# Two-layer hybrid backbone on one core: the token shift of the RWKV in-projection by transfers inside SBUF and one blend, low-rank weights padded to 128 rows

## The chip, the cores and the metric

One core of a Trainium2 chip runs the whole program in one launch. The metric is the device time of one execution in microseconds; lower is better. The work runs on TensorE (PE in the rows, its weight loads PEld), VectorE (DVE), ScalarE (ACT), GpSimd (POOL), and the DMA engines, which are fed mostly from SyncE's queue (SP). Each engine, and SP's queue too, takes its instructions strictly in the order of the program.

## What is computed

1024 latent tokens (a grid of 16 rows of 64) and 256 context tokens pass through two layers. The first has an in-projection of 1024 to 3840 channels; its first 2560 columns are mixed with a shifted copy of themselves, and this mixing is what the change rewrites:

```python
def qshift(u, rows):                       # latent tokens
    g = u.reshape(b, rows, GRID_W, ch // 4, 4)
    left  = jnp.pad(g[:, :, :-1, :, 0], ...)   # channel 0 of 4: neighbour to the left
    right = jnp.pad(g[:, :, 1:, :, 1], ...)    # channel 1: to the right
    up    = jnp.pad(g[:, :-1, :, :, 2], ...)   # channel 2: one grid row up
    down  = jnp.pad(g[:, 1:, :, :, 3], ...)    # channel 3: one grid row down
...
        s = (s + (shift_fn(s) - s) * mu).astype(jnp.float32)
        r, k0, v, wl_f, wl_b, al_f, al_b = jnp.split(s, cuts, axis=-1)
...
    w_log = -jax.nn.softplus(-(w0 + jnp.tanh(wl) @ w2)) - 0.5
    a = jax.nn.sigmoid(a0 + al @ a2)
```

The context uses the same with two classes of channels (previous and next token). Channels lie on the partitions, tokens along the free axis, so a class of channels is every fourth (or every second) partition and a shift is an offset along the row. The low-rank inputs `wl`, `al` have 64 channels for each of the two directions.

## The kernel before

The first part of the program (phase A, up to about 590 us) is the in-projection. A tile of 128 output channels is one product: 8 steps of 9 matmuls (three operand splits of fp32 into two parts, three blocks of 256, 512 and 512 tokens; lines 546 to 553). Two PSUM tiles of such a product are live at a time (pool `pg`). `gemm(plan)` (in `phaseA`) issues a product and, after the steps that the plan names, work for other tiles; this plan fixes the order on every engine by hand.

The order of products is: 18 and 19 (the low-rank inputs), 28, 29 (gates), 26, 27 (Fourier), then for each of six pairs of heads p the tiles k, v, r; then the last gates. For a pair, in the loop at the end of `phaseA` (`P` is the new pair, `old` the one before):

- in the product of the new k: `old.take(0, pr)` mixes r, then `operands(0, 0)`, `operands(0, 1)` build the forward operands of the state update, `values` turns v by TensorE (`pvt`, line 757, copied by ACT at 758) and stores it to DRAM in six transfers (lines 763 to 765);
- in the product of v (`VPL`): `B` splits the low-rank weights (`wsplit`: `hw`, `ha` on ACT, then `lw`, `la` on VectorE, line 727) and mixes k (`take(1, k)`); `l` issues low-rank products (`lora`, lines 779 and 780, their tanh on ACT at 781); `q` is `square` (ACT, line 740), `o` are the backward operands `operands(1, .)`. Then `norm` (matmuls `pn`, line 746) reads the squares;
- in the product of r (`RPL`): more `lora`, `b` the bonus (`pbo`, line 866, multiplied on VectorE at 867), `t` mixes v (`take(2, v)`), `T` and `S` send the norms through DRAM (`RN`, line 792) and back spread over the partitions (`kk`, line 800), which `keys` multiplies at 806.

`norm`, `lora` and the bonus share two PSUM buffers (`gen`), so `pbo` can start only when `rn` (VectorE, line 748) has read `pn`. On VectorE `rn` stands behind all of `operands(1, .)`. On ACT `square` stands ahead of the exponentials `Pp`, `Pi` (832, 833) of `operands(1, .)`.

`mix` (line 560) takes a product from PSUM: two ACT instructions write `m = (1 - mu) * u` (564, 565), then six VectorE passes add `mu` times the shifted PSUM tile, each with a column of multipliers (`muc`) that is zero outside one class of channels (line 575). For the low-rank inputs ACT also copies the PSUM tile to `u` first (568, 569), and the passes read that. `lowrank` then applies the tanh (for 18 only) and `stacked` splits the tile into two parts (ACT 540, VectorE 541).

A `lora` product is `wh` (both halves of the 128 partitions hold the 64 rows of a direction, 128 rows) times the stacked input, plus the rest `wl` of the weights (64 rows, `w[hs, :]`) times one half of the input (lines 779, 780).

Around the low-rank inputs SP also loads 1 MB pieces of the modulation weights (`aw`, line 314) with two small loads each (line 320); product 29 is followed by matmuls on these pieces (`pada`, line 331) in the two `gen` buffers, which ACT empties into `adap` (333). In ACT's order the split of `AL` (540), two weight casts (528) and the gate of product 28 (590, 591) stand ahead of these copies.

Weights of a product come in two halves of 256 KB (`wr`, line 521), each loaded two halves ahead. The build gives the DMAs of SP's queue eight semaphores in turn; each DMA waits until the one issued eight before it has landed.

Of the kernel before, what the change touches and what calls it, by code (L numbers as in the profile page):

```python
# [18 lines left out]
T = 1280  # L19
# [27 lines left out]
KT = 4  # L47
# [34 lines left out]
def host_consts():  # L82
# [16 lines left out]
    c["cls"] = np.stack([t % 4 == 0, t % 4 == 1, t % 4 == 2, t % 4 == 3, t % 2 == 0, t % 2 == 1], 1)  # L99
# [114 lines left out]
def setup(g, es):  # L214
    nc, tc = g.nc, g.tc
    cp = es.enter_context(tc.tile_pool(name="cp", bufs=1, reuse_waits="tile"))
    g.cp = cp
    es.enter_context(tc.manual_schedule())
    load_consts(g, ["cols", "ident"], cp)
    c = g.K["cols"]  # L220
    g.col = lambda n: c[:, COLS[n][0] : COLS[n][0] + COLS[n][1]]
    mh = cp.tile([128, 1], F32, name="mhalf")
    nc.gpsimd.memset(mh, -0.5)
    g.K["mhalf"] = mh
    one = cp.tile([128, 1], F32, name="one")
    nc.gpsimd.memset(one, 1.0)
    g.K["one"] = one
    g.dv = cp.tile([128, 6 + 6 + 6 + 6 + 12 + 12 + 20 + 120], F32, name="dv")
    g.ap = cp
    g.shc = cp.tile([128, 2, 8, 2], F32, name="shc")  # L230
    g.scc = cp.tile([128, 2, 8, 2], F32, name="scc")


def derived(g):
# [5 lines left out]
    def sl(n):  # L240
# [186 lines left out]
def front(g, A, load, split, steps):  # L427
# [3 lines left out]
    with ExitStack() as es:  # L431
# [3 lines left out]
        for t in range(10):  # L435
# [8 lines left out]
            if t == 1:  # L444
                load_consts(g, ["cls", "sel2"], g.cp)
                derived(g)
                ada_setup(g, A.wp)
# [255 lines left out]
class Pair:  # L703
# [63 lines left out]
    def lora(self, d):  # L767
# [104 lines left out]
def phaseA(g, B=None):  # L872
# [72 lines left out]
    load_consts(g, ["fch", "selh", "onesbd", "mscan"], g.lp)  # L945
# [29 lines left out]
    load_consts(g, ["fctx"], g.fp)  # L975
# [10 lines left out]
    v = gemm({i: [some(F1, 1)] for i in range(1, 7)})  # L986
# [4 lines left out]
    for p in range(g.npair + 1):  # L991
        P = P if not p else Pair(g, p) if p < g.npair else None
        if old:
            val, bon = old.values(), old.bonus()
            first = lambda: (old.take(0, pr), old.kdir())
            k = gemm({0: [first], 4: [lambda: old.operands(0, 0), some(val, 1)], 5: [some(val, 1)], 6: [lambda: old.operands(0, 1), some(val, 2)]})
        if P:
            lo0, lo1, keys = P.lora(0), P.lora(1), P.keys()
        if not old:
# [3 lines left out]
            pr = gemm({0: [lambda: P.take(2, v)], 1: [some(lo0, 2)], 2: [some(lo0, 2)], 3: [some(lo0, 2)], KT: [P.turned, some(lo1, 2)], KF: [P.spread, some(lo1, 2)], 6: [some(lo1, 2)], 7: [some(keys, 4)]})  # L1003
        elif P:
            def act(a, n):
                return {"B": lambda: (P.wsplit(), P.take(1, k)), "l": some(lo0, n), "q": P.square, "o": lambda: old.operands(1, n), "u": old.sum_dirs, "p": old.store_pc, "b": some(bon, n)}[a]
# [3 lines left out]
            def act(a, n):  # L1010
                return {"l": some(lo1, n), "b": some(bon, n), "k": some(keys, n), "t": lambda: P.take(2, v), "T": P.turned, "S": P.spread}[a]
# [1206 lines left out]
```

## Time and profile before

| | us |
|---|---|
| three runs | 1917.75, 1933.57, 1937.59 (median 1933.57) |
| the profiled execution | 1926.12 |
| its span, first to last instruction | 1924.3 |
| TensorE busy in it | 1779.5 (92%) |
| VectorE busy in it | 1128.5 (59%) |
| ScalarE, GpSimd busy | 716.3, 693.8 |
| mean granted TensorE clock | 0.970 of full speed |

Times in the rows are microseconds from the span's start, mean durations of one instruction are ns where a row says so. A busy TensorE is not one at its peak: its ends are modelled, and only the spacing of starts tells the rate.

### The profile page before, as it was taken

The numbers are of one execution on the slowest core, as the hardware profiler recorded it, in microseconds if no ns is written. First come the engines' busy times: TensorE is split into PE (matmuls) and PEld (weight loads), VectorE is DVE, ScalarE is ACT, GpSimd is POOL, SyncE is SP. The second block draws the span as 40 slices with busy tenths as digits, with TensorE's granted clock in tenths as the row PEclk, the third lists the DMA queues.
The fourth block names the chain that finished last, engine by engine and source line by source line (L and its number), as shares of the span: only waits on it lengthen the run. The fifth ranks groups of instructions, "written<-read, shape, count | busy, mean of one in ns | idle before, by whom it ended". The sixth has DMA issues, their size and how long they took to land. (4 is left out here: it accounts for less than half of the span.)

```text
span 1924.3 us, 38535 instructions
## 1 busy us (share of the span) xinstructions
PE 1779.5 (92%) x15490; PEld 1487.0 (77%) x15490; DVE 1128.5 (59%) x2030; ACT 716.3 (37%) x1598; POOL 693.8 (36%) x826
## 2 busy tenths in 40 slices
PE   6999998999889888989998787999999999999998
PEld 4777776677668777778877676779889898898876
DVE  5532578887884656977888754554352533423643
ACT  5322554544441133455555565343221222212231
POOL 4331334443442414554565522122342424413310
PEclk9999999999999988999999898999999999999999
DMA  9671265556568385678767764433111101101162
GB/s 314 174 238 51 80 173 141 153 141 167 147 164 253 105 187 147 172 176 202 186 181 169 198 178 139 145 123 107 36 56 34 49 30 45 55 34 55 50 202 99
DMA packets 341494, 257.60 MB, mean 134 GB/s; under 512 B 109964, under 2 KB 292740, under 8 KB 341060
## 3 DMA queue, kind: packets, MB, share of 16 engines
q1 hardware_dynamic: 326756, 221.96, 42.3%
q10 hardware_dynamic: 10512, 18.62, 3.2%
q0 software_dynamic: 4048, 14.55, 2.0%
q8 instruction: 123, 2.02, 0.5%
q14 instruction: 55, 0.45, 0.1%
HBM read 175.20 MB, written 79.88 MB: 133 GB/s over the span
## 5 line engine op out<-in xcount | busy, mean ns | idle before, releaser
L552 PE MATMUL pgm<-hh,wh 128*128 128x512 f32 (+1 forms) x624 | 172.9, 386 | 0.0
L530 POOL TENSOR_TENSOR wl<-wr,wh 128x512 fp32r<-128x512 f32 x60 | 85.5, 1430 | 210.3 <-ACT wh L528 190.1
L552 PE MATMUL pgm<-hl,wh 128*128 128x512 f32 (+1 forms) x624 | 160.5, 366 | 0.0
L552 PE MATMUL pgm<-hh,wl 128*128 128x512 f32 (+1 forms) x624 | 159.8, 365 | 0.0
L1138 PE MATMUL psc<-arr,bkp 128*128 128x128 f32 x960 | 136.2, 290 | 9.8 <-DMA bkp<-scr_BK 5.1
L1138 PEld LDWEIGHTS psc<-arr,bkp 128*128 128x128 f32 x960 | 118.5, 196 | 17.9 <-DVE scr L1139 9.1
L552 PEld LDWEIGHTS pgm<-hl,wh 128*128 128x128 f32 x624 | 106.4, 194 | 20.0 <-POOL hl L488 0.9
L552 PEld LDWEIGHTS pgm<-hh,wl 128*128 128x128 f32 x624 | 106.6, 194 | 19.5
L552 PEld LDWEIGHTS pgm<-hh,wh 128*128 128x128 f32 x624 | 99.3, 193 | 27.5 <-issue 14.6
L1872 PE MATMUL pv<-wv,hh 128*128 128x256 f32 x640 | 117.2, 285 | 0.0
L575 DVE SCALAR_TENSOR_TENSOR m<-pgm,dv,m 128x255 f32<-128x255 f32 (+2 forms) x108 | 105.1, 987 | 12.5 <-ACT m L565 9.8
L1139 DVE TENSOR_TENSOR scr<-psc,mask 128x512 f32<-128x512 f32 x120 | 81.8, 685 | 43.3 <-PE psc L1138 42.7
L1872 PEld LDWEIGHTS pv<-wv,hh 128*128 128x128 f32 x640 | 99.5, 192 | 0.1
L1192 DVE TENSOR_TENSOR td<-z,tl 128x70 f32<-128x70 f32 (+40 forms) x248 | 85.0, 343 | 23.0 <-DMA tl<-dn 17.2
L1507 POOL TENSOR_TENSOR state<-tmp,pc 128x256 f32<-128x256 f32 x46 | 36.8, 801 | 167.2 <-DVE tmp L1502 127.1
L1195 DVE TENSOR_TENSOR z<-z,td 128x70 f32<-128x70 f32 (+40 forms) x248 | 88.4, 357 | 8.5
L1438 ACT COPY wt<-ws 64x256 f32<-64x256 f32 x120 | 44.0, 366 | 127.3 <-PE ws L1433 117.7
L1872 PE MATMUL pv<-wv,hl 128*128 128x256 f32 x320 | 90.5, 283 | 0.0
L1611 PE MATMUL pow_eo<-w_eo,yhw_eo 128*128 128x512 f32 x320 | 89.6, 401 | 0.5 <-ACT w_eo L1577 0.4
L1192 POOL TENSOR_TENSOR tp<-z,tl 128x24 f32<-128x24 f32 (+22 forms) x189 | 78.1, 413 | 12.4
L1195 POOL TENSOR_TENSOR z<-z,tp 128x24 f32<-128x24 f32 (+22 forms) x189 | 76.9, 407 | 14.8
L1433 PE MATMUL ws<-vu,scr 128*64 128x64 f32 x960 | 49.5, 230 | 27.4 <-DVE vu L1506 12.4
(339 smaller groups left out, 4286.6 us busy)
## 6 DMA issues: line engine op xcount, KB each, us to landing
aw<-ada_w SPq DMA_DIRECT2D x16, 1024.0 KB, 11.5
wr<-w_ev SPq DMA_DIRECT2D x60, 256.0 KB, 4.2
scr_AR<-ar SPq DMA_DIRECT2D x24, 640.0 KB, 3.8
scr_BK<-bk SPq DMA_DIRECT2D x24, 640.0 KB, 4.5
arr<-scr_AR SPq DMA_DIRECT2D x60, 256.0 KB, 3.8
bkp<-scr_BK SPq DMA_DIRECT2D x120, 128.0 KB, 4.4
br<-scr_BK ACTq DMA_DIRECT2D x60, 256.0 KB, 3.9
x<-xin SPq DMA_DIRECT2D x20, 512.0 KB, 4.4
```

The costliest lines, as they stand in the source:

```text
L530: nc.gpsimd.tensor_tensor(out=wl, in0=wr, in1=wh.bitcast(F32), op=ALU.subtract)
L552: g.nc.tensor.matmul(ps[:, b, :n], lhsT=st[:, k % 4, :], rhs=mv[:, k, c0 : c0 + n], start=(k == 0 and i == 0), stop=(k == 7 and i == 2))
L575: nc.vector.scalar_tensor_tensor(out=o, in0=i, scalar=g.muc[:, q, ft : ft + 1], in1=o, op0=ALU.mult, op1=ALU.add)
L1138: mm(ps[:, 128 * x : 128 * x + 128], lhsT=BK[s][:, h, x, :], rhs=AR[s][:, x, :], start=True, stop=True)
L1139: tt(out=sc[:, :, h].rearrange("p (d q) t -> p d q t", q=2), in0=ps.rearrange("p (d q t) -> p d q t", q=2, t=128), in1=K["mask2"].unsqueez ...
L1192: eng.tensor_tensor(out=tv, in0=Z[:, ra - r0 : rb - r0, s : s + 1].broadcast_to([U, k, n]), in1=TL[:, s : s + 1, s + 1 : 32].broadcast_to( ...
L1195: eng.tensor_tensor(out=zo, in0=zo, in1=tv, op=ALU.add)
L1433: mm(WS[H[h], 64 * x : 64 * x + 64], lhsT=sc[:, x, h, 0:64], rhs=vu[:, x, h], start=True, stop=True, tile_position=(0, 64 * h))
L1438: nc.scalar.copy(WT2[H[h], h].rearrange("p x v -> p (x v)"), WS[H[h], 0:256])
L1507: (nc.vector if SE[0] <= s < SE[1] or s >= SE[2] else nc.gpsimd).tensor_tensor(out=STS[1 - s % 2], in0=tmp, in1=pc.broadcast_to([128, 4, 6 ...
L1611: self.g.nc.tensor.matmul(ps[:, 512 * b : 512 * b + 512], lhsT=st[:, k, :], rhs=mv[:, 512 * b : 512 * b + 512], start=(k == 0 and i == 0), ...
L1872: mm(ps[:, 256 * e : 256 * e + 256], lhsT=st[:, k, c0 : c0 + 128], rhs=mv[:, k, :], start=(k == 0 and i == 0), stop=(k == 7 and i == 2))
```

## The change

`mix` now copies the product from PSUM to `m` unscaled (ACT, two instructions), and six DMAs on SP's queue move the classes of channels, shifted, from `m` into one tile `sh` (128 partitions, 1280 columns, one buffer for all mixes): two of 32 partitions with 16 pieces of 63 elements (252 bytes), two of 32 partitions with 960 elements, two of 64 partitions with 255 elements. A new function `blend` then forms `m = m * (1 - mu)` and `m = sh * mu + m` in two VectorE instructions over 1280 columns. For the pairs `blend` is placed some steps behind `take` (`x` in the plans); for the low-rank inputs it follows at once. `sh` is cleared once, so its borders stay zero.

The rest weights `lw`, `la` become tiles of 128 rows for each direction, cleared once; `wsplit` writes the 64 rows of a direction, and the matmul at line 780 reads all 128 rows. The constant `cls` and the multipliers `muc` go, `fch` is loaded later, and the scratch for DMA descriptors is set to 8192.

```diff
-RPL = {2:"l1",3:"b4 t",4:"l1",5:"T l1",6:"S l2",7:"l1 k4"}
+RPL = {2:"l1",3:"b4 t",4:"l1",5:"T l1 x",6:"S l2",7:"l1 k4"}
-VPL = {0:"B",2:"l2",3:"l2",4:"l2 q o0",5:"u",6:"o1 p"}
+VPL = {0:"B",2:"l2 x",3:"l2",4:"l2 q o0",5:"u",6:"o1 p"}
...
-def mix(g, ps, ft, m, u=None):
+def mix(g, ps, ft, m):
+    nc, sh = g.nc, g.SH
+    pc, pl = ps
+    nc.scalar.copy(m[:, 256:T], pl)
+    nc.scalar.copy(m[:, 0:256], pc)
+    def rows(t, q, n=4):
+        return t[q::n]
+    def grid(t, q):
+        return rows(t, q)[:, 256:T].rearrange("p (r w) -> p r w", w=64)
+    move = nc.sync.dma_start
+    move(grid(sh, 0)[:, :, 1:64], grid(m, 0)[:, :, 0:63])
+    move(grid(sh, 1)[:, :, 0:63], grid(m, 1)[:, :, 1:64])
+    move(rows(sh, 2)[:, 320:T], rows(m, 2)[:, 256 : T - 64])
+    move(rows(sh, 3)[:, 256 : T - 64], rows(m, 3)[:, 320:T])
+    move(rows(sh, 0, 2)[:, 1:256], rows(m, 0, 2)[:, 0:255])
+    move(rows(sh, 1, 2)[:, 0:255], rows(m, 1, 2)[:, 1:256])
+def blend(g, ft, m):
     nc = g.nc
...
-    add(mc[:, 1:256], pc[:, 0:255], 4)
-    add(mc[:, 0:255], pc[:, 1:256], 5)
-    add(mlr[:, :, 1:64], plr[:, :, 0:63], 0)
-    add(mlr[:, :, 0:63], plr[:, :, 1:64], 1)
-    add(ml[:, 64:1024], pl[:, 0:960], 2)
-    add(ml[:, 0:960], pl[:, 64:1024], 3)
+    nc.vector.tensor_scalar(out=m, in0=m, scalar1=g.omm[:, ft : ft + 1], scalar2=None, op0=ALU.mult)
+    nc.vector.scalar_tensor_tensor(out=m, in0=g.SH, scalar=g.col("mu")[:, ft : ft + 1], in1=m, op0=ALU.mult, op1=ALU.add)
...
-            wl = g.sm.tile([128, 128], F32R, tag="l" + n, name=f"l{n}_{self.p}", bufs=1)
+            wl = g.LW[n]
...
-                nc.vector.tensor_tensor(out=wl[a], in0=w[a], in1=wh[a, d].bitcast(F32), op=ALU.subtract)
+                nc.vector.tensor_tensor(out=wl[a, d], in0=w[a], in1=wh[a, d].bitcast(F32), op=ALU.subtract)
...
-                nc.tensor.matmul(pa[:, :bn], lhsT=w[hs, :], rhs=src[hs, b0 : b0 + bn], start=False, stop=True)
+                nc.tensor.matmul(pa[:, :bn], lhsT=w[:, d], rhs=src[:, b0 : b0 + bn], start=False, stop=True)
...
     def lowrank(ps, ft, nm):
         m = g.mp.tile([128, T], F32, tag=f"m{ft % 2}", name=f"m{ft}")
-        mix(g, ps, ft, m, g.mp.tile([128, T], F32, tag="m2", name=f"u{ft}"))
+        mix(g, ps, ft, m)
+        blend(g, ft, m)
...
-            k = gemm({0: [first], 4: [lambda: old.operands(0, 0), some(val, 1)], 5: [some(val, 1)], 6: [lambda: old.operands(0, 1), some(val, 2)]})
+            k = gemm({0: [first], 2: [lambda: old.blend(0)], 4: [lambda: old.operands(0, 0), some(val, 1)], 5: [some(val, 1)], 6: [lambda: old.operands(0, 1), some(val, 2)]})
...
-    nc = bacc.Bacc("TRN2", target_bir_lowering=False, num_devices=1)
+    nc = bacc.Bacc("TRN2", target_bir_lowering=False, num_devices=1, dynamic_dma_scratch_size=8192)
```

The first place is SP's queue where one pair's forward operands and values are stored (`scr_BK`, `scr_VT`; `wr` are halves of weights). Before, the two loads of weights follow the values, whose three rows stand twice in a row:

```order
L850 DMA scr_BK<-bk_0_1_2426 128x10x128
L763 DMA scr_VT<-vt_2386 640x1x128
L764 DMA scr_VT<-vt_2386 64x2x128
L765 DMA scr_VT<-vt_2386 64x8x128
L521 DMA wr_0_2454<-w_ev 128x512
L521 DMA wr_1_2540<-w_ev 128x512
L849 DMA scr_AR<-ar_1_0_2573 128x10x128
```

In the changed program the six moves of `take(1, k)` (the tile `m_2_2492` of pair 2) stand at the same place:

```order
L850 DMA scr_BK<-bk_0_1_2435 128x10x128
L764 DMA scr_VT<-vt_2395 640x1x128
L765 DMA scr_VT<-vt_2395 64x2x128
L766 DMA scr_VT<-vt_2395 64x8x128
L516 DMA wr_0_2463<-w_ev 128x512
L569 DMA sh<-m_2_2492 32x16x63
L570 DMA sh<-m_2_2492 32x16x63
L571 DMA sh<-m_2_2492 32x960
L572 DMA sh<-m_2_2492 32x960
L573 DMA sh<-m_2_2492 64x255
L574 DMA sh<-m_2_2492 64x255
L516 DMA wr_1_2549<-w_ev 128x512
```

The moves have come in behind the stores of the forward operands and of the values, and between the two halves of weights.

The second place is VectorE at the same time of the same pair (`lw`, `la` the rests of the weights, `m_2` the mixed k, `Pi_1_0` the first of the backward operands). Before:

```order
L727 TENSOR_TENSOR lw_2_2470<-w_2_2291,hw_2_2469 64x128 x2
L727 TENSOR_TENSOR la_2_2478<-a_2_2293,ha_2_2477 64x128 x2
L575 SCALAR_TENSOR_TENSOR m_2_2485<-pgm_2295,dv,m_2_2485 128x255 x2
L575 SCALAR_TENSOR_TENSOR m_2_2485<-pgm_2295,dv,m_2_2485 128x16x63 x2
L575 SCALAR_TENSOR_TENSOR m_2_2485<-pgm_2295,dv,m_2_2485 128x960 x2
L831 SCALAR_TENSOR_TENSOR Pi_1_0_2566<-mscan,sg_1_2184 128x256
```

And now:

```order
L726 TENSOR_TENSOR lw_697<-w_2_2298,hw_2_2478 64x128 x2
L726 TENSOR_TENSOR la_698<-a_2_2300,ha_2_2485 64x128 x2
L579 TENSOR_SCALAR m_2_2492<-m_2_2492,dv 128x1280
L580 SCALAR_TENSOR_TENSOR m_2_2492<-sh,cols,m_2_2492 128x1280
L831 SCALAR_TENSOR_TENSOR Pi_1_0_2575<-mscan,sg_1_2189 128x256
```

Six passes became two instructions at the same place of the order: nothing stands between the rests of the weights and the blend, and the backward operands still stand behind it.

The third place is SP's queue at the low-rank input `AL` (`aw`, `adbb`, `adnb` are the modulation weights and their small loads). Before:

```order
L314 DMA aw_11_868<-ada_w 128x8x256
L320 DMA adbb_11_870<-ada_b 128x256
L320 DMA adnb_11_872<-npost 128x256
L521 DMA wr_0_941<-w_ev 128x512
L521 DMA wr_1_983<-w_ev 128x512
```

And now (`m_922` is the tile of product 19):

```order
L309 DMA aw_11_868<-ada_w 128x8x256
L315 DMA adbb_11_870<-ada_b 128x256
L315 DMA adnb_11_872<-npost 128x256
L569 DMA sh<-m_922 32x16x63
L570 DMA sh<-m_922 32x16x63
L571 DMA sh<-m_922 32x960
L572 DMA sh<-m_922 32x960
L573 DMA sh<-m_922 64x255
L574 DMA sh<-m_922 64x255
L516 DMA wr_0_940<-w_ev 128x512
```

The moves of the low-rank input stand behind the last of four loads of 1 MB, where before came weights of later products; counted back eight places from line 574 stands the load `aw_11`.

## Rows read from the trace of the kernel before

**Rows 1.** Busy us (instructions) of each engine, TensorE's clock, DMA share, GB/s

```profile
65.00:170.00 105.00, 103.41 (x594) 79.65 (x593) 38.53 (x55) 29.40 (x46) 29.43 (x47) 1.00 0.49 159
...
270.00:334.00 64.00, 59.18 (x279) 44.66 (x278) 52.57 (x59) 31.13 (x53) 26.89 (x20) 0.97 0.56 151
```

**Rows 2.** What TensorE waited for, 165 to 600 us: total, times, longest

```profile
PE pa L780 <- DVE lw L727: 11.2, 5, 2.9
...
PE pbo L866 <- DVE rn L748: 2.5, 2, 1.3
```

**Rows 3.** The page's costliest groups: the passes of the mixing

```profile
L575 DVE SCALAR_TENSOR_TENSOR m<-pgm,dv,m 128x255 f32<-128x255 f32 (+2 forms) x108 | 105.1, 987 | 12.5 <-ACT m L565 9.8
```

**Rows 4.** VectorE's groups by shape, 0 to 70 and 165 to 600

```profile
L463 DVE TENSOR_SCALAR x<-x,ss 128x1024 f32<-128x1024 f32 x10 | 7.5, 752 | 0.3 <-POOL ss L373 0.3
...
L859 DVE SCALAR_TENSOR_TENSOR kd<-kd,cols,m 128x1280 f32<-128x1280 f32 x6 | 9.2, 1538 | 0.0
```

**Rows 5.** TensorE's timeline: start, duration, instruction, count

```profile
320.85 0.75 PE L552 MATMUL pgm<-hl,wh 128*128 128x256 f32 x3
...
321.43 0.75 PE L552 MATMUL pgm<-hh,wl 128*128 128x256 f32 x3
...
340.09 0.48 PE L779 MATMUL pa<-WL,hw 128*128 128x512 f32 x1
...
340.50 0.49 PE L780 MATMUL pa<-WL,lw 64*128 64x512 f32 x1
...
340.93 0.85 PE L552 MATMUL pgm<-hh,wh 128*128 128x256 f32 x3
```

**Rows 6.** SP's timeline behind one pair's forward operands

```profile
307.05 0.36 SPq L850 DMA_DIRECT2D scr_BK<-bk  x1
...
315.00 1.58 SPq L521 DMA_DIRECT2D wr<-w_ev  x2
```

**Rows 7.** Stretches of the DMA engines: TensorE's clock, DMA share, GB/s

```profile
308.00:312.00 4.00, 0.61 1.01 246
...
318.00:319.00 1.00, 1.00 0.81 272
...
319.00:320.00 1.00, 1.00 0.14 49
...
604.00:606.00 2.00, 1.00 0.77 169
```

**Rows 8.** DMA issues: count, KB each, us from issue to landing

```profile
dn<-scr SPq DMA_DIRECT2D x60, 128.0 KB, 3.4
```

**Rows 9.** The 1 MB loads of modulation weights (line 314)

```profile
DMA to landing us min/median/max: 8.6/11.5/14.9
```

**Rows 10.** The same pair's timeline on VectorE and ScalarE

```profile
308.21 5.98 DVE L575 SCALAR_TENSOR_TENSOR m<-pgm,dv,m 128x255 f32<-128x255 f32 x6
...
317.33 1.35 ACT L740 ACTIVATE sq<-m,cols 128x1280 f32<-128x1280 f32 x1
...
318.58 0.73 ACT L832 ACTIVATE Pp<-Pi 128x640 f32<-128x640 f32 x1
...
319.40 0.96 DVE L843 TENSOR_TENSOR ar<-kk,Pp 128x256 f32<-128x256 f32 x1 [3.44 <-issue]
...
333.68 0.16 DVE L748 TENSOR_SCALAR rn<-pn 128x20 f32<-128x20 f32 x1
```

**Rows 11.** The timeline around the low-rank input AL

```profile
97.11 5.99 DVE L575 SCALAR_TENSOR_TENSOR m<-u,dv,m 128x255 f32<-128x255 f32 x6
...
101.41 2.84 SPq L314 DMA_DIRECT2D aw<-ada_w  x1
...
103.18 2.54 ACT L540 CAST AL<-m 64x1280 fp32r<-64x1280 f32 x2 [10.10 <-DVE m L575]
...
108.45 0.38 SPq L320 DMA_DIRECT2D adnb<-npost  x1
...
111.05 0.37 ACT L333 COPY adap<-pada 128x256 f32<-128x256 f32 x1 [2.23 <-PE pada L331]
```

More of the change, by code (lines that the diff above doesn't have):

```diff
@@ L227, in setup @@
     g.K["one"] = one
-    g.dv = cp.tile([128, 6 + 6 + 6 + 6 + 12 + 12 + 20 + 120], F32, name="dv")
+    g.dv = cp.tile([128, 6 + 6 + 6 + 6 + 12 + 12 + 20], F32, name="dv")
     g.ap = cp
@@ L444, in front @@
             if t == 1:
-                load_consts(g, ["cls", "sel2"], g.cp)
+                load_consts(g, ["sel2"], g.cp)
                 derived(g)
@@ L734, in take, with blend @@
         setattr(self, "rkv"[q], m)
+    def blend(self, q):
+        blend(self.g, 6 * q + self.p, getattr(self, "rkv"[q]))
     def square(self):
@@ L772, in lora @@
         sgd = pp.tile([128, T], F32, tag="sg", name=f"sg{p}_{d}", bufs=2)
-        hs = slice(64 * d, 64 * d + 64)
         self.th.append(thd)
         self.sg.append(sgd)
-        for src, w, wh, dst, bias in ((g.WL[d], self.wl[0], self.wh[0], sgd, g.w0h), (g.AL[d], self.wl[1], self.wh[1], thd, g.a0h)):
+        for src, w, wh, dst, bias in ((g.WL[d], g.LW["w2"], self.wh[0], sgd, g.w0h), (g.AL[d], g.LW["a2"], self.wh[1], thd, g.a0h)):
             for b0, bn in BL:
@@ L944, in phaseA @@
     A.load(2)
-    load_consts(g, ["fch", "selh", "onesbd", "mscan"], g.lp)
+    load_consts(g, ["selh", "onesbd", "mscan"], g.lp)
+    g.LW = {n: g.lp.tile([128, 2, 128], F32R, name="l" + n) for n in ("w2", "a2")}
+    for t in g.LW.values():
+        nc.gpsimd.memset(t.bitcast(F32), 0.0)
+    g.SH = g.lp.tile([128, T], F32, name="sh")
+    nc.gpsimd.memset(g.SH, 0.0)
     def lowrank(ps, ft, nm):
         m = g.mp.tile([128, T], F32, tag=f"m{ft % 2}", name=f"m{ft}")
-        mix(g, ps, ft, m, g.mp.tile([128, T], F32, tag="m2", name=f"u{ft}"))
+        mix(g, ps, ft, m)
+        blend(g, ft, m)
         if ft == 18:
@@ L974, in phaseA @@
     g.fp = e2.enter_context(tc.tile_pool(name="fp", bufs=1, reuse_waits="tile"))
-    load_consts(g, ["fctx"], g.fp)
+    load_consts(g, ["fch", "fctx"], g.fp)
     g.K["flat"] = g.fp.tile([128, 2, 4, 512], F32, name="flat")
@@ L985, in phaseA @@
     P.take(1, k)
-    v = gemm({i: [some(F1, 1)] for i in range(1, 7)})
+    v = gemm({i: [lambda: P.blend(1)] * (i == 2) + [some(F1, 1)] for i in range(1, 7)})
     e2.close()
@@ L1002, in phaseA @@
             P.norm()
-            pr = gemm({0: [lambda: P.take(2, v)], 1: [some(lo0, 2)], 2: [some(lo0, 2)], 3: [some(lo0, 2)], KT: [P.turned, some(lo1, 2)], KF: [P.spread, some(lo1, 2)], 6: [some(lo1, 2)], 7: [some(keys, 4)]})
+            pr = gemm({0: [lambda: P.take(2, v)], 1: [some(lo0, 2)], 2: [some(lo0, 2), lambda: P.blend(2)], 3: [some(lo0, 2)], KT: [P.turned, some(lo1, 2)], KF: [P.spread, some(lo1, 2)], 6: [some(lo1, 2)], 7: [some(keys, 4)]})
         elif P:
             def act(a, n):
-                return {"B": lambda: (P.wsplit(), P.take(1, k)), "l": some(lo0, n), "q": P.square, "o": lambda: old.operands(1, n), "u": old.sum_dirs, "p": old.store_pc, "b": some(bon, n)}[a]
+                return {"B": lambda: (P.wsplit(), P.take(1, k)), "l": some(lo0, n), "x": lambda: P.blend(1), "q": P.square, "o": lambda: old.operands(1, n), "u": old.sum_dirs, "p": old.store_pc, "b": some(bon, n)}[a]
             v = gemm({k_: [act(a[0], int(a[1:] or 0)) for a in x.split()] for k_, x in VPL.items()})
@@ L1010, in act @@
             def act(a, n):
-                return {"l": some(lo1, n), "b": some(bon, n), "k": some(keys, n), "t": lambda: P.take(2, v), "T": P.turned, "S": P.spread}[a]
+                return {"l": some(lo1, n), "b": some(bon, n), "k": some(keys, n), "t": lambda: P.take(2, v), "x": lambda: P.blend(2), "T": P.turned, "S": P.spread}[a]
             plan = {k: [act(a[0], int(a[1:] or 0)) for a in x.split()] for k, x in RPL.items()}
```

21 lines of the change are left out of this document (1 added, 20 removed).

## Prediction, made before the changed kernel was run

> **What bounds the kernel now.** I read the busy time by stretch first, then TensorE's waits, then the orders of work on VectorE and on SP's queue beside their timelines, then the DMA engines by stretch. In the stretch of the low-rank inputs TensorE is busy 103.41 of 105 us: whatever delays it there is paid in full. In one pair's period of 64 us it is busy 59.18 us and VectorE 52.57 us [rows 1]; neither is full, so a pair is set by a chain that crosses engines. The waits show where it closes: TensorE waits for the rests of the low-rank weights, 11.2 us in five waits, and in the bonus for `rn`, 2.5 us in two [rows 2]. Both stand on VectorE behind a long stretch of operands and mixes. That a VectorE instruction is short therefore helps only if the chain through its place in the queue gets shorter.
>
> **The mixing on VectorE.** Six passes of 987 ns go, 5.92 us for a tile [rows 3]. The blend has a scaling of 1280 columns, for which 752 ns on 1024 columns gives 0.94 us, and a second instruction like the 1.54 us one of the same shape [rows 4]: 2.48 us. So 3.44 us of VectorE's time go for each of 20 tiles. ACT keeps two instructions of the same sizes; I cost that at nothing, since it is 31 of 64 us busy [rows 1]. The cleared tiles, the later `fch` and the dropped constants come once, beside loads; nothing, and 2 us if that cover is gone. The smaller descriptor scratch has no row to price it; I take nothing, and leave a few us to the range.
>
> **The transfers.** The passes read PSUM directly. Now six DMAs move one tile's worth, 655 KB. At the rate of a full stretch, 246 GB/s, that is 2.7 us; at the 169 GB/s of a stretch that holds the 256-byte pieces of the `dn` stores it is 3.9 us [rows 7]. I take 3.2, between them, since 40% of the bytes are such pieces. An unhindered transfer of 512 such pieces lands 3.4 us after its issue [rows 8], so one mix alone waits some 6 us where the passes took 5.92: about even. What decides is what stands ahead of the moves in SP's queue.
>
> Here a rule of the Trainium skill speaks against the change: "DMA: Bandwidth & Descriptors", Specifications, wants pieces of 512 bytes or more and says that below this a read-modify-write is made. By it the 252-byte pieces (258 KB of a tile) would cost about double, 1 to 1.5 us more for a tile on the path, some 6 us in all as an estimate. The landing of the 256-byte stores does not show such a doubling, and my sum leaves it out.
>
> **One pair, step by step.** The mix of k is the costly one, for its moves stand behind the stores of the forward operands and the values. Those keep the DMA engines full: share 1.01 from 308 to 312, still 0.81 in 318 to 319, then 0.14 [rows 7], so the backlog ends near 319.0. It holds two halves of weights, issued from 315.00 [rows 6]; one of them, 256 KB or 1.05 us at 246 GB/s, now follows the moves. So the moves run from 317.9 to 320.6 at best and 321.8 at worst, I take 321.5 with the completion; the blend ends at 324.0. The passes ended at 308.21 + 5.98 = 314.19 [rows 10]. The k tile is 9.8 us later.
>
> Queued behind it on VectorE are all backward operands, behind its reader `square` on ACT their exponentials, and TensorE waits for `square` in `norm`. In the kernel before VectorE had 3.44 us of idle time just there, up to 319.40, for `Pp`, which ended at 319.31 [rows 10]. Now it follows `square` (1.35 us) and `Pp` (0.73 us): 326.1. So 6.7 of the 9.8 us remain. From there to `rn` at 333.68 [rows 10] VectorE works through, and TensorE needs `rn` for the buffer of the bonus: the bonus is 6.7 us later.
>
> Between `rn` and the next pair's mix of r two things change. The low-rank products are shorter: a pair of matmuls of 512 columns, 128 and 64 rows, starts at 340.09 and ends with the next product's start at 340.93, 0.84 us, where 1280 columns of the main product take 0.58 us, so 0.46 us for twice 512 [rows 5]. That is 0.38 us for each, up to 4.6 us for twelve in a pair (3.0 if the four of 256 columns gain nothing; I take 4). Five of them lie behind the bonus, 1.5 to 1.9 us; the others run while VectorE is late and are hidden. Against it, the round trip of the norms (`RN`, `kk`) stands behind the moves of v in the queue, 2.7 to 3.9 us later, and `keys` and the mix of r wait for it. Net -1.5 to +0.5 us; I take -0.5. The waits for the rests of the weights stay as they are, since those follow the same operands. A period grows by 6.7 - 0.5 = 6.2 us, from 4.3 (cheap moves, -1.5) to 8.4 (dear ones, landing late, +0.5). It comes five times, for the k of pairs 1 to 5: 31 us. Pair 0 has no values ahead of its moves and keeps its low-rank gain: -4 us, bounds -4.6 and 0.
>
> **The low-rank input AL.** Its moves follow the last 1 MB load of modulation weights, and the sixth must wait until that load has landed, by the eight semaphores. The load is issued at 101.41 [rows 11] and such loads land after 8.6 to 14.9, median 11.5 us [rows 9]: 112.9. The sixth move lands 3.4 us later, the blend ends at 118.8, where the passes ended at 103.10. Behind the blend on ACT stand the split of `AL`, two casts, a gate and then `adap`, which frees TensorE's buffers. `adap` came 7.95 us behind the passes, 2.23 of them idle for TensorE [rows 11], so 5.7 us are ACT's and VectorE's own. Now it comes at 124.5 instead of 111.05: 13.4 us, from 10.6 to 16.9 by the two ends of the landing, and TensorE has nothing else in its queue. The moves of the other low-rank input meet no such load just ahead and end about with the old passes: nothing, up to 3 us if the weights of product 29 come late.
>
> **The sum.** On the profiled execution's 1926.12 us: 13.4 + 31 - 4 = +40.4, 1966.5. The median of the runs, 1933.57, stands 7.5 us above that execution; from it the same step gives 1974. I forecast 1968. By the bounds of the terms it lies between 1926 + 10.6 + 21.5 - 4.6 = 1954 and 1926 + 16.9 + 42 + 0 = 1985. About 1% is what a measurement of this kernel can tell from no change, 1914 to 1953.
>
> **The rivals.** First, faster: the moves are hidden, because VectorE's queue would have stood idle there anyway, and TensorE sets the pair. Then a period loses the low-rank gain of 4 to 4.6 us, six times, 24 to 28 us: near 1900. For it: TensorE's 59.18 of 64 us. Against it: VectorE has only 3.44 us of idle time at the place where 9.8 are added. It decides if the moves of k land before about 314.
>
> Second, about the same: the delay of `rn` is taken up by the 4.8 us that TensorE is not busy in a period [rows 1] and by the 4 us of shorter products, so periods stay at 64 us, and only the low-rank input costs: 1926 + 13.4 - 4 = 1935. Against it: that idle time lies in front of `rn` and the rests, at the end of this same chain.
>
> Third, slower still: the padding gains nothing, because a matmul's time does not depend on its rows, and the 0.84 us come from the two-step accumulation. Then pair 0 keeps its 4 us and each period loses about 1 us more: 1966.5 + 4 + 5 = 1975.5. For it speaks only that both halves of a pair start late, 0.41 and 0.43 us [rows 5]. The Trainium skill says this in "TensorE: Matmul & The Clock Gate", Why this matters for your kernels: a matmul of few rows takes the time of a full one. The spacing in the trace disagrees, as the main product's matmuls of 128 rows run at 0.23 us for 512 columns.
>
> **How the numbers follow.** Forecast 0.62, first rival 0.15, second 0.13, third 0.10. Faster by over 1% is the first: 0.15. Within 1% are the second and the lowest end of the forecast, 0.03: 0.16. Slower: 0.69. The range leaves out the first rival and the ends of the bounds: 1920 to 1990. The likeliest case's own is 1954 to 1985.
>
> **What would show it.** Right: VectorE's idle time in front of line 579 for k, some 10 us in each of five pairs, ended by a DMA; TensorE waiting at `pn` for `square` and at `pbo` for `rn`; `adap` near 124 us; pairs some 70 us apart; a pair of low-rank matmuls spaced 0.46 us. Wrong: the moves of k landing before 317, or TensorE passing `pn` without a wait, would put the pairs' term down; `adap` near 111 would take out the first term.

## The result, and the profile after

Four runs of the changed kernel took 1984.43 to 1993.39 us, median 1986.38, beside 1933.02 for the kernel before: a ratio of 1.0302, with a 95% interval of 1.0248 to 1.0357. By the ratio that is 58 us slower (53 by the medians): on the side that was forecast, beyond the size of 40 and beyond 1985, the upper end of the prediction's bounds. The profiled execution is the longest of the four, span 1991.6 us.

First the low-rank inputs and one pair's period (busy time by stretch; engines PE, PEld, DVE, ACT, POOL, then TensorE's granted clock, DMA share, GB/s):

```profile
65.00:178.00 113.00, 97.53 (x568) 75.55 (x566) 29.11 (x46) 24.36 (x39) 29.04 (x48) 0.94 0.47 157
290.00:363.00 73.00, 59.98 (x277) 49.40 (x277) 44.87 (x47) 30.57 (x53) 28.25 (x19) 0.88 0.58 158
```

A pair takes 73 us where it took 64 [rows 1], with TensorE busy for nearly as long (59.98 and 59.18 us) and 8 us less work for VectorE: neither engine's work sets the period, but what they wait for. TensorE's waits, 165 to 600 us (total, times, longest):

```profile
PE pn L747 <- ACT sq L741: 33.2, 5, 7.1
PE pvt L758 <- ACT vt L759: 22.8, 5, 5.3
PE pbo L866 <- DVE rn L749: 5.2, 5, 1.3
PE pa L780 <- DVE lw L726: 1.9, 3, 0.8
```

`pn` now waits for `square` in each of the five pairs, as forecast, and the wait for the rests of the weights [rows 2] has shrunk from 11.2 to 1.9 us. Ahead of it TensorE now waits for the copies `vt`, 22.8 us where it was 7.7. VectorE's wait stands in the page's group of the blend (busy, mean ns, idle before):

```profile
L579 DVE TENSOR_SCALAR m<-m,dv 128x1280 f32<-128x1280 f32 x20 | 19.5, 973 | 153.4 <-DMA sh<-m 131.9
```

The timeline shows where: first AL, then the period that follows `rn` at 290.18 (start, duration, instruction, idle time before it and what ended it; SPq rows are issues on SP's queue).

```profile
116.25 0.89 DVE L579 TENSOR_SCALAR m<-m,dv 128x1280 f32<-128x1280 f32 x1 [21.05 <-DMA sh<-m]
...
118.81 2.54 ACT L535 CAST AL<-m 64x1280 fp32r<-64x1280 f32 x2 [29.09 <-DVE m L580]
...
124.32 0.66 ACT L328 COPY adap<-pada 128x256 f32<-128x256 f32 x2
...
290.18 0.17 DVE L749 TENSOR_SCALAR rn<-pn 128x20 f32<-128x20 f32 x1
...
305.49 6.06 POOL L816 TENSOR_TENSOR kd<-kd,m 128x1280 f32<-128x1280 f32 x2 [1.32 <-ACT kd L815]
...
307.47 6.31 DVE L806 SCALAR_TENSOR_TENSOR kk<-m,cols,kk 128x256 f32<-128x256 f32 x3 [4.68 <-DMA kk<-scr_RN]
313.70 0.88 DVE L579 TENSOR_SCALAR m<-m,dv 128x1280 f32<-128x1280 f32 x1
...
329.08 0.59 DVE L726 TENSOR_TENSOR lw<-w,hw 64x128 fp32r<-64x128 f32 x2
...
329.63 0.62 SPq L764 DMA_DIRECT2D scr_VT<-vt  x1
...
330.03 0.40 PE L779 MATMUL pa<-WL,hw 128*128 128x512 f32 x1
330.26 0.39 PE L780 MATMUL pa<-WL,lw 128*128 128x512 f32 x1
330.49 0.74 PE L547 MATMUL pgm<-hh,wh 128*128 128x256 f32 x3
...
337.82 1.40 SPq L569 DMA_DIRECT2D sh<-m  x1
...
341.89 0.59 SPq L574 DMA_DIRECT2D sh<-m  x1
...
344.05 0.89 DVE L579 TENSOR_SCALAR m<-m,dv 128x1280 f32<-128x1280 f32 x1 [13.74 <-DMA sh<-m]
...
346.45 1.53 DVE L831 TENSOR_TENSOR_SCAN Pi<-mscan,sg 128x256 f32<-128x256 f32 x2
346.56 1.36 ACT L741 ACTIVATE sq<-m,cols 128x1280 f32<-128x1280 f32 x1 [9.54 <-DVE m L580]
...
363.15 0.17 DVE L749 TENSOR_SCALAR rn<-pn 128x20 f32<-128x20 f32 x1
```

`adap` comes at 124.32 for 111.05 [rows 11]. The moves of k are issued only behind the stores of the values, the first at 337.82 and the sixth at 341.89; VectorE stands idle 13.74 us. A pair of low-rank matmuls of 512 columns takes 0.46 us, 330.03 to 330.49, for 0.84 [rows 5]. What was not forecast is at 307.47: three instructions of `keys` take 6.31 us. In the kernel before they took 2.42, and there GpSimd's two products `kd` (line 816) began only at their end; now they run side by side. The same step of the same pair before:

```profile
269.68 0.17 DVE L748 TENSOR_SCALAR rn<-pn 128x20 f32<-128x20 f32 x1
...
284.60 2.42 DVE L806 SCALAR_TENSOR_TENSOR kk<-m,cols,kk 128x256 f32<-128x256 f32 x3 [4.45 <-DMA kk<-scr_RN]
...
286.91 5.88 POOL L816 TENSOR_TENSOR kd<-kd,m 128x1280 f32<-128x1280 f32 x2 [1.50 <-ACT kd L815]
...
292.83 2.61 DVE L831 TENSOR_TENSOR_SCAN Pi<-mscan,sg 128x384 f32<-128x384 f32 x2
...
306.95 0.59 DVE L727 TENSOR_TENSOR lw<-w,hw 64x128 fp32r<-64x128 f32 x2
```

Counted from `rn` to `rn`, the five periods grew from 73.06, 64.00, 62.51, 64.05 and 64.83 us to 80.11, 72.97, 73.12, 72.53 and 73.69, together by 44.0 us, and the first `rn` came 13.45 us later (210.07 for 196.62). The two make 57.4 of the 67.3 us between the two profiled executions. The other 10 lie behind the last `rn`: 1.7 in the operands of the last pair, the rest in later parts that the change does not touch; this execution is the longest of its four.

### The profile page after: what moved, and what is told of

Read it like the earlier page. It is cut to its first block, busy times and chain, and to the rows that moved or that the text cites. A ratio compares the mean times of both kernels' runs of the same rounds, so it can differ in the third digit from the quotient of the medians.

```text
span 1991.6 us, 38669 instructions
## 1 busy us (share of the span) xinstructions
PE 1786.1 (90%) x15490; PEld 1511.9 (76%) x15490; DVE 1070.6 (54%) x1949; ACT 710.0 (36%) x1594; POOL 699.5 (35%) x829
## 5 line engine op out<-in xcount | busy, mean ns | idle before, releaser
L547 PEld LDWEIGHTS pgm<-hh,wh 128*128 128x128 f32 x624 | 107.4, 203 | 21.1 <-issue 6.2
L579 DVE TENSOR_SCALAR m<-m,dv 128x1280 f32<-128x1280 f32 x20 | 19.5, 973 | 153.4 <-DMA sh<-m 131.9
L840 POOL TENSOR_TENSOR ar<-m,Pp 128x640 f32<-128x640 f32 (+2 forms) x30 | 37.1, 1245 | 143.1 <-ACT Pp L832 138.4
```

What stands on the lines that cost most here:

```text
L547: g.nc.tensor.matmul(ps[:, b, :n], lhsT=st[:, k % 4, :], rhs=mv[:, k, c0 : c0 + n], start=(k == 0 and i == 0), stop=(k == 7 and i == 2))
L840: nc.gpsimd.tensor_tensor(out=ar[:, cs, 64:128], in0=ch(proc(self.r, d, lo, n)), in1=Pp[:, cs, 1:65], op=ALU.mult)
```

## Experiments

Each ratio is against the kernel before, run on the same chip, with its 95% interval; 0.001 is 1.9 us. The changed kernel's own ratio is known to 0.005 only, so a difference to it of less than some 0.007 (13 us) is not clear by the time alone; there the traces decide. From the first `rn` to the last, the changed kernel takes 372.4 us, and e12 and e4, which leave the pairs' order as it is, 371.1 and 371.5; the kernel before takes 328.4, and e7 and e11, whose edits turned out to do nothing, 327.5 and 334.5.

**The queue ahead of the moves.** Two runs change only the order of issue. In one the stores of the values go behind the moves of k:

```diff
-            k = gemm({... 6: [lambda: old.operands(0, 1), some(val, 2)]})
+            k = gemm({... 6: [lambda: old.operands(0, 1), some(val, 1)]})
-VPL = {0:"B",2:"l2 x",3:"l2",4:"l2 q o0",5:"u",6:"o1 p"}
+VPL = {0:"B s",2:"l2 x",3:"l2",4:"l2 q o0",5:"u",6:"o1 p"}
...
```

`s` is the last step of `values`, the six stores.

> The changed kernel with the six stores of the turned values issued behind the moves of k instead of ahead of them. They are 1.31 MB, 5.3 us at 246 GB/s. Theory (what stands ahead of the moves in SP's queue and in the DMA engines decides): blend of k 4 to 6 us earlier in each of five pairs, about 20 to 27 us less than the changed kernel, near 1963. Rival (the moves are slow by themselves, their small pieces take 6 us from issue to landing whatever stands ahead; or the stores only push the same delay onto the weights): less than 6 us gained, 1980 or more.

Measured: 1.0185 (1.0152 to 1.0219), 23 us less than the changed kernel; the four later periods are 66.6 to 68.4 us. In the other, AL's copies and moves go ahead of the modulation loads:

```diff
+    ml = shift(a, 19)
     ada(4, 4)
-    g.AL = lowrank(a, 19, "AL")
+    g.AL = lowrank(ml, 19, "AL")
...
```

> The changed kernel with the copies and moves of the low-rank input AL issued ahead of the modulation loads that follow product 28, the blend left where it was. Theory (the sixth move waits for the 1 MB load ahead of it): VectorE's wait for AL's moves goes, adap comes near 112 instead of 124.3, rn of pair 0 near 198, and 12 to 13 us less than the changed kernel, near 1973. Rival (the loads come later instead, or the delay is taken up before pair 0): less than 4 us.

Measured: 1.0256 (1.0236 to 1.0275), 9 us less; `rn` of pair 0 at 200.91, 9.2 us earlier. TensorE no longer waits for `adap` (14.9 us in the changed kernel) but, in this run's waits from 65 to 165 us, for the loads that now come later:

```profile
PE pada L326 <- DMA aw<-ada_w: 4.7, 2, 3.9
```

So the theory holds for 9 of the 13 us, and its rival for the other 4. Both orders together:

> The changed kernel with both orders changed: stores of the turned values behind the moves of k, and AL's moves ahead of the modulation loads. The two alone gave 1.0185 and 1.0256 where the changed kernel has 1.0302. Theory (two separate stretches): they add, 1.012 to 1.016. Rival: one takes the other's gain, 1.018. Neither can beat the kernel before, since r's and k's moves stay on the path.

Measured: 1.0126 (1.0080 to 1.0173); 22.6 and 8.9 us alone, 34 together. The two terms are separate, and still the kernel is slower than before. With the moves on ScalarE's queue:

```diff
-    move = nc.sync.dma_start
+    move = nc.scalar.dma_start
```

> The changed kernel with the six moves issued by ScalarE instead of SyncE, right behind the copies. Theory (their place behind the stores in SP's queue costs): the moves share the DMA engines with the stores instead of following them, blend of k 3 to 6 us earlier, 15 to 25 us less than the changed kernel if ScalarE's issues cost nothing there; AL's too, since the moves no longer stand behind the 1 MB load, 10 to 13 us more. Rival (the DMA engines are full, so the queue does not matter, and ScalarE pays some 0.6 us for each of 120 issues): 1980 or slower.

Measured: 1.0498 (1.0483 to 1.0514), slower by another 38 us: the rival, and by more than its 0.6 us for each issue. ScalarE takes its instructions in order, and with the DMA engines full (share 0.96 from 336 to 342 us, 0.94 to 346) it stands at the issue of its own moves (its timeline, ACTq are issues):

```profile
335.78 0.66 ACTq L569 DMA_DIRECT2D sh<-m  x1
...
344.39 1.09 ACTq L574 DMA_DIRECT2D sh<-m  x1
345.53 1.05 ACT L781 ACTIVATE sg<-pa,dv 128x256 f32<-128x256 f32 x2 [9.51 <-DMA sh<-m]
```

The tanh of the low-rank products wait 9.51 us behind them, and TensorE waits for those, 53.5 us in nine waits. What the moves lose by standing behind the stores is less than what ScalarE loses by issuing them.

**The size of the pieces.** The two moves of 252-byte pieces as one piece for each partition:

```diff
-    move(grid(sh, 0)[:, :, 1:64], grid(m, 0)[:, :, 0:63])
+    move(rows(sh, 0)[:, 257:T], rows(m, 0)[:, 256 : T - 1])
```

> The changed kernel with the 252-byte pieces of two moves made into one piece of 4092 bytes for each partition; the borders of the grid rows then take a wrong neighbour. Theory (small pieces cost no more than their bytes): the moves take the same, within 4 us of 1986 to 1992, ratio to the kernel before 1.027 to 1.032. Rival (pieces under 512 bytes cost double): 1 to 1.5 us for each of six or seven tiles on the path, 6 to 10 us less, ratio near 1.026.

Measured: 1.0312 (1.0271 to 1.0353): no gain, nor in the five periods (371.1 us for 372.4). From issue to landing the moves of short pieces take 4.2 us, those of long ones 4.0 (medians of 40). The rule of 512 bytes that the prediction weighed (the Trainium skill, "DMA: Bandwidth & Descriptors", Specifications) shows no price in these transfers inside SBUF.

**No moves at all.** Without the six transfers only the other parts of the change are left:

```diff
-    move(grid(sh, 0)[:, :, 1:64], grid(m, 0)[:, :, 0:63])
...
-    move(rows(sh, 1, 2)[:, 0:255], rows(m, 1, 2)[:, 1:256])
```

> The changed kernel with the six transfers of each tile left out: sh stays zero, so the shifted part of the mixing is missing. Theory (all that the change costs is the wait for the transfers, in the stretch of AL and for k of each pair, and the collision of keys with GpSimd's products that their lateness makes): the padding and the shorter blends are left as gains, 1895 to 1912, keys back to 2.4 us. Rival (the plain copies, the blend's place in the queues or a lower clock carry the cost): 1940 or more.

Measured: 0.9964 (0.9944 to 0.9983). The moves and all that hangs on them thus cost 65 us, yet the rest of the change, 3.44 us less for VectorE on each tile and shorter products, gave 7 us: a median of 1918.76, where 1895 to 1912 were expected. `keys` took up to 8 us in this run too.

**The collision on VectorE.** Padding alone, on the kernel before (with `fch` loaded later, as in the change), shows the same:

```diff
-                nc.tensor.matmul(pa[:, :bn], lhsT=w[hs, :], rhs=src[hs, b0 : b0 + bn], start=False, stop=True)
+                nc.tensor.matmul(pa[:, :bn], lhsT=w[:, d], rhs=src[:, b0 : b0 + bn], start=False, stop=True)
```

> The kernel before with the rest weights padded to 128 rows and nothing else of the change. Theory (a period is set by VectorE's chain, so the shorter low-rank products count only in pair 0 and behind the bonus): 4 us in pair 0 and 1.7 us in each of five periods, 12 us less than the kernel before, near 1920. Rival A (TensorE sets the period): all of 4 to 4.6 us six times, 24 to 28 us less, near 1907. Rival B (a matmul's time does not depend on its rows): the same as before, 1933, with pairs of 512 columns still spaced 0.84 us.

Measured: 0.9991 (0.9970 to 1.0013), nothing; but not by any of the three ways. The periods are 68.28, 62.55, 67.04, 66.99 and 66.40 us: 4.8 and 1.5 us gained, then 1.6 to 4.5 lost. The fourth, on GpSimd and VectorE:

```profile
410.31 6.07 POOL L815 TENSOR_TENSOR kd<-kd,m 128x1280 f32<-128x1280 f32 x2 [1.49 <-ACT kd L814]
...
410.43 8.20 DVE L805 SCALAR_TENSOR_TENSOR kk<-m,cols,kk 128x256 f32<-128x256 f32 x3 [5.13 <-DMA kk<-scr_RN]
```

The products follow the end of r's product, which shorter low-rank matmuls bring forward; `keys` follow the round trip of the norms, which they don't. The products start 0.12 us ahead of `keys` and run beside them. The kernel before is not safe from this either: in e7 (the smaller scratch alone) `keys` came late once (16.29 us behind `rn` for some 14.9) and took 4.53 us. A wait that holds them behind `keys`, with and without the padding:

```diff
+        nc.gpsimd.tensor_copy(out=self.pc[:, 0, 0:1], in_=self.kk[:, T - 1 : T])
         for d in range(2):
             t2 = g.pt.tile([128, T], F32, tag="t2", name=f"kd{p}_{d}", bufs=2)
```

> The kernel before with the padding and with GpSimd's products behind keys. The padded one alone gained 4.8 and 1.5 us in its first two periods and lost 2 to 4.5 us in the next three, where its keys took 6 to 8 us. Theory (the padding brings the products onto keys, and this gives its gain back): all periods 62 to 63 us, ratio to the kernel before 0.988 to 0.994, near 1914. Rival (the padding's gain is lost to something else, as TensorE's waits for the copies vt and a lower clock behind them): ratio 0.998 to 1.002.

> The kernel before with the products behind keys and no padding: what the wait alone does. Theory: nothing, for there the products come behind keys by themselves; ratio 0.998 to 1.002, so that the gain of the padded kernel with this wait is the padding's. Rival: 0.994 too, the padding then has no part in it.

Measured: 0.9940 (0.9920 to 0.9959) with the padding, periods 68.27, 60.90, 63.08, 60.93 and 62.54 us, and 1.0009 (0.9989 to 1.0030) without. The padding is worth 0.6%, but only if its product does not bring the collision. This version, without any of the moves, is faster than both kernels. Its timeline:

```profile
403.37 1.81 DVE L805 SCALAR_TENSOR_TENSOR kk<-m,cols,kk 128x256 f32<-128x256 f32 x3 [4.28 <-DMA kk<-scr_RN]
405.10 5.98 DVE L575 SCALAR_TENSOR_TENSOR m<-pgm,dv,m 128x255 f32<-128x255 f32 x6
...
405.38 5.88 POOL L816 TENSOR_TENSOR kd<-kd,m 128x1280 f32<-128x1280 f32 x2
```

The products now run beside the passes, and the passes take their 5.98 us. In the kernel before it was so too. Two tables of VectorE's groups by shape in that kernel, for the passes beside the products (286 to 294 us) and for those of v (400 to 407), beside which GpSimd has only a split of weights, up to 402.5:

```profile
L575 DVE SCALAR_TENSOR_TENSOR m<-pgm,dv,m 128x1008 f32<-128x1008 f32 x2 | 2.5, 1264 | 0.0
...
L806 DVE SCALAR_TENSOR_TENSOR kk<-m,cols,kk 128x512 f32<-128x512 f32 x2 | 1.4, 741 | 0.0
...
L575 DVE SCALAR_TENSOR_TENSOR m<-pgm,dv,m 128x1008 f32<-128x1008 f32 x2 | 2.5, 1263 | 0.0
```

1264 and 1263 ns: a pass, which has one operand in PSUM, takes no longer beside the products. `keys` and the second instruction of the blend have both in SBUF. The same wait in the changed kernel shows what that does:

> The changed kernel with GpSimd's two products kd made to wait until VectorE has done keys, by a copy of one column of kk at the head of kdir. Theory (keys run beside those products and take 5 to 7 us for three instructions instead of 2.4, and all forward operands, the stores and the moves of k stand behind them): keys back to 2 to 3 us, each of five periods 2.5 to 4 us shorter, 1966 to 1974. Rival (the moves of k come when the stores let them, keys are not on the path): within 5 us of the changed kernel's 1986. Rival 2 (the products come too late for the operands): slower than 1986.

Measured: 1.0374 (1.0359 to 1.0389), 14 us slower than the changed kernel: slower, as the second rival said, but not for its reason, for the operands wait for the blend and not for the products. `keys` are back at 1.81 us, but the blend of r, which the change put in the place of the passes, now meets the products:

```profile
305.93 1.81 DVE L806 SCALAR_TENSOR_TENSOR kk<-m,cols,kk 128x256 f32<-128x256 f32 x3 [4.83 <-DMA kk<-scr_RN]
...
307.94 6.41 POOL L817 TENSOR_TENSOR kd<-kd,m 128x1280 f32<-128x1280 f32 x2
...
309.95 1.63 DVE L579 TENSOR_SCALAR m<-m,dv 128x1280 f32<-128x1280 f32 x1 [2.21 <-DMA sh<-m]
311.62 4.08 DVE L580 SCALAR_TENSOR_TENSOR m<-sh,cols,m 128x1280 f32<-128x1280 f32 x1
```

1.63 and 4.08 us, where alone they take 0.88 and 1.55. The first of them has one tensor operand only and grows all the same, to 3.64 us at worst (e8): two operands in SBUF are not a condition for it. Issuing the products ahead of `keys` did not free them either (`d` is `kdir`):

```diff
-RPL = {2:"l1",3:"b4 t",4:"l1",5:"T l1 x",6:"S l2",7:"l1 k4"}
+RPL = {2:"l1",3:"b4 t",4:"l2",5:"T l1 x",6:"S l2 d",7:"k4"}
...
```

> The changed kernel with GpSimd's two products kd (and ScalarE's two instructions ahead of them) issued in the product of r, ahead of keys, and one low-rank product moved two steps earlier so that their input is there. Theory (what the collision of these products with VectorE's instructions on SBUF costs lies on the path, whether it falls on keys, 6.3 us for 2.4, or on the blend of r as with the products behind keys): they now fall into VectorE's wait for kk, 4.7 us, keys take 2 to 3 us and the blend of r 2.4, each of five periods 3 to 4 us shorter, 1966 to 1973. Rival (the moves of k set the period whatever comes before): within 5 us of 1986 to 1992.

> The kernel before with the padding and the same early place of the products. Theory: keys stay near 2 us, as with the products behind keys (ratio 0.994), and the six passes, which read PSUM and were not slower beside the products, stay at 6 us: 0.990 to 0.996. Rival (the two ScalarE instructions ahead of the copies of r delay the passes): 0.998 or more.

Measured: 1.0275 (1.0234 to 1.0317) and 1.0017 (0.9998 to 1.0036). In both `keys` still took 3.9 to 6.5 us: the products began some 12 us behind `rn` instead of 15.3 to 15.5, and were still running when `keys` came, with GpSimd's splits of weights (`wl`) right behind them. These two decide nothing. So the products were left out, in the changed kernel and in the one without moves:

```diff
-            nc.gpsimd.tensor_tensor(out=t2, in0=t2, in1=self.k, op=ALU.mult)
```

> The changed kernel with GpSimd's two products kd left out (the keys of the state update then lack the factor k): nothing runs beside VectorE on SBUF at keys and at the blend of r. Theory (the collision makes the step from rn to the end of the blend of r 3 to 4 us longer, and this is what the forecast's -0.5 us for that step missed): keys 2 us, blend of r 2.4 us, periods 73 to 69.5 us, ratio to the kernel before 1.020 to 1.024. Rival (the stores and moves of k set the period): 1.027 to 1.032.

> The kernel with the moves left out, and the two products as well (the shifted part and the factor k are missing). Without the moves alone the periods were 62.8 us and the ratio 0.996, where the shorter blends and the padding should have given more. Theory (keys took 4.5 to 8 us there by the same collision): periods 59 to 60 us, ratio 0.983 to 0.988. Rival (TensorE's waits at the copies vt and the lower clock behind them hold the period): 0.993 to 0.998.

Measured: 1.0239 (1.0192 to 1.0285) and 0.9832 (0.9783 to 0.9880), 12 and 25 us less than with the products. The periods are 76.83, 71.06, 70.22, 70.64 and 71.06 us in the first, 65.17 and 56 to 59 in the second. One period of the first:

```profile
285.40 0.17 DVE L749 TENSOR_SCALAR rn<-pn 128x20 f32<-128x20 f32 x1
...
303.03 2.85 DVE L806 SCALAR_TENSOR_TENSOR kk<-m,cols,kk 128x256 f32<-128x256 f32 x3 [5.00 <-DMA kk<-scr_RN]
306.76 0.89 DVE L579 TENSOR_SCALAR m<-m,dv 128x1280 f32<-128x1280 f32 x1 [0.88 <-DMA sh<-m]
...
322.19 0.60 DVE L726 TENSOR_TENSOR lw<-w,hw 64x128 fp32r<-64x128 f32 x2
...
339.75 1.53 DVE L830 TENSOR_TENSOR_SCAN Pi<-mscan,sg 128x256 f32<-128x256 f32 x2
```

By the time alone the first is not clear of the changed kernel; by its five periods it is, 359.8 us for 371.1 to 372.4. Nothing else was waiting for the products: in the changed kernel they end at 311.55, and their result is first read at 321.21 (line 848).

**The padding in the changed kernel, and the scratch.** The rest product on 64 rows again in the changed kernel, and the smaller scratch in the kernel before:

```diff
-                nc.tensor.matmul(pa[:, :bn], lhsT=w[:, d], rhs=src[:, b0 : b0 + bn], start=False, stop=True)
+                nc.tensor.matmul(pa[:, :bn], lhsT=w[hs, d], rhs=src[hs, b0 : b0 + bn], start=False, stop=True)
```

```diff
-    nc = bacc.Bacc("TRN2", target_bir_lowering=False, num_devices=1)
+    nc = bacc.Bacc("TRN2", target_bir_lowering=False, num_devices=1, dynamic_dma_scratch_size=8192)
```

> The changed kernel with the rest product on 64 rows again, as before the change. Theory: pair 0 loses its 4 us and each period the products behind the bonus, 1.7 us: 12 us more than the changed kernel, near 1998. Rival A (TensorE sets the period of the changed kernel too): 24 to 28 us more, near 2012. Rival B (padding gains nothing, or is all hidden): 1986.

> The kernel before with the descriptor scratch of 8192 alone. Theory: it costs nothing, 0.998 to 1.002. Rival: it is part of the 58 us, 1.003 or more.

Measured: 1.0364 (1.0332 to 1.0395), 12 us slower than the changed kernel, as the theory said (by the five periods 9.6 us, 3.4 of them in the first); and 0.9994 (0.9964 to 1.0024), nothing.

## Why the prediction was right and wrong

**Right: the bound.** A pair was taken to be a chain across engines, in which VectorE's waits count and its busy time does not. VectorE lost 8 us of work in a period that became 9 us longer.

**Right: AL.** `adap` was put at 124.5 and came at 124.32; 13.4 us were forecast and the first `rn` came 13.45 later. e4 shows the loads ahead in the queue to be the cause of 9 of these 13 us. That the two agree to 0.1 us is chance: in runs with nothing changed up to there, the first `rn` came from 196.62 to 199.45 in the kernel before (e7, e11) and from 208.57 to 210.56 in the changed one (e15, e13).

**Right: k.** The blend of k was to end 9.8 us after the passes it replaces, less 0.5 from the step before: 9.3. With the products left out the scan behind it starts 54.35 us after `rn` (339.75 - 285.40), where it started 44.43 us after (314.11 - 269.68): 9.9. In the changed kernel it is 11.8, for the reason below. e3 shows that the stores ahead of the moves make most of it: there the blend ends 10.1 us behind the start of `lw` in the second period, where the changed kernel has 17.5 and the passes had 7.2. VectorE then catches up 2.9 us before `rn` (16.70 us from the scan on for 19.57), where 3.1 were read.

**Wrong: "Net -1.5 to +0.5 us; I take -0.5"**, the step from `rn` to the blend of r. By the place where the forward operands end (`lw`): 37.27 us after `rn` before (306.95 - 269.68), 38.90 after (329.08 - 290.18), so +1.6. The two parts that the step names were about right: `kd`, at the end of r's product, starts 15.31 us after `rn` for 17.23, 1.9 us earlier, and `keys` 17.29 for 14.92, 2.4 later. But these two alone add up to a loss (1.5 to 1.9 us against 2.7 to 3.9), and the prediction does not say how -0.5 comes from them. And a third part was missing: `keys` come later behind the moves of v, the products earlier by the shorter low-rank matmuls, and they collide, 6.31 us for 2.42. Over the five periods the run without the products is 12.6 us shorter (372.4 and 359.8 us), of the 17 by which 44.0 exceeds the 27 forecast. Without them the step takes 36.79 us (322.19 - 285.40), which is the -0.5; this is in part luck, for the scan behind the mix of r, which met the products in the kernel before (2.61 us), takes 1.53 there.

A page could have warned of it: the Trainium skill says in "SBUF — State Buffer", Who interferes with whom, that a VectorE instruction with two SBUF inputs contends with a GpSimd instruction that reads SBUF, and that one with at most one SBUF input does not, outside the modes that use both of VectorE's ports, in which it counts `tensor_scalar`. The traces agree: 6.31 and 2.42 us for `keys`, 1264 and 1263 ns for the passes, and 1.63 for 0.88 us for the blend's `tensor_scalar` with its one SBUF input, though no run shows in which mode that one ran.

**Wrong: "one mix alone waits some 6 us where the passes took 5.92: about even"**, which carried the 4 us gained in pair 0. For r of pair 0 in the changed kernel:

```profile
232.54 0.64 SPq L569 DMA_DIRECT2D sh<-m  x1
...
235.87 0.59 SPq L574 DMA_DIRECT2D sh<-m  x1
...
238.12 2.66 DVE L579 TENSOR_SCALAR m<-m,dv 128x1280 f32<-128x1280 f32 x1 [4.08 <-DMA sh<-m]
240.81 2.47 DVE L580 SCALAR_TENSOR_TENSOR m<-sh,cols,m 128x1280 f32<-128x1280 f32 x1
```

The blend starts 5.6 us after the first issue; SP needs 0.54 to 0.64 us for each of the six issues, which the 3.4 us of an unhindered transfer did not hold. With the blend, 5.1 us beside GpSimd's work, that is 10.7 for 5.9. The padding's 4 us are there (e1 gained 4.8 in that period) and are eaten here: `lw` comes 46.46 us after the first `rn`, where it came at 46.31, and 43.21 without the products, so the collision takes 3.25 of them. The first period grew by 7.05 us where 6.2 - 4 were forecast, and by 3.8 without the products.

Over the five periods the traces account for the 17 us so: the steps from `rn` to `lw` came 13.6 us dearer than forecast, the products' 12.6 among them; from `lw` to the end of the mix of k it is 0.7 us; and VectorE caught up 2.6 us less behind it: 2.9 us in four periods and 1.35 in the third, where the 3.1 read in one pair were put for each. Two small readings were off without weight in the sum: the six moves carry 634 KB by their shapes, not 655, and the waits for the rests did not stay as they were but fell to 1.9 us.

**The rivals.** The padding does gain something (e2 and e9), against the third. Its pair still accumulates in two steps and now takes 0.46 us, so these are not what the 0.84 us came from; why 64 rows cost more stays open. The moves were not hidden, against the first. A gain of its size shows only with the moves and the products both left out (0.9832, 32 us); as that also takes away work of GpSimd and a collision that the kernel before has, it is not shown to be the padding's.

## What to carry to other kernels

Moving work from VectorE to transfers exchanges busy time, which may cost nothing, for a place in a queue; read what stands ahead in that queue, bytes and issues, at each place where the result is waited for. Before an operand changes from PSUM to SBUF, or an instruction slides by a few microseconds, look at what GpSimd does at that moment. A gain that appears to be nothing, as the padding's, may be a gain and a collision: compare the periods one by one, not the total.

## What was not expected of the hardware

VectorE instructions on SBUF grow two- to fourfold and more beside GpSimd's products (`keys` 1.81 us alone in e9, 8.20 at worst in e1; the blend's first instruction 0.88 to 3.64 in e8, its second 1.55 to 4.15 in e6), while the passes, with one operand in PSUM, do not. GpSimd slows less: one product takes 2.97 us, and 4.30 at worst (e13). Six transfers take 4 to 5 us to issue on one queue, even with nothing ahead: 232.54 to 236.5 for pair 0. And a wait came with the lower clock: behind the wait for `pn`, in which TensorE stood 6.58 us up to 347.98, it was granted 1.2 GHz:

```profile
350.00:356.00 6.00, 6.00 (x23) 5.42 (x23) 6.00 (x7) 0.00 (x0) 3.75 (x3) 0.50 0.02 6
```

What that costs was not measured. It can be little here: `rn`, which ends the period, stands behind VectorE's operands, and VectorE idles only 0.8 us in all between 344.05 and 363.15.
